# An mLSTM and sparse-attention trunk: two small products of the row scale early in the second unit, block-diagonal products behind the evacuations

## The chip, the cores and the metric

The kernel runs on one core of one Trainium2 chip. The metric is device microseconds of one execution of the whole program, from one launch. Three runs of the kernel before took 384.11, 388.54 and 380.40 us. All inputs and the output lie in device memory; the host only rearranges the weights ahead of the launch.

## The reference, cut

Two layers over 256 tokens of 1024 channels, batch 1: an mLSTM layer and a sparse-attention (NSA) layer, then a final norm. The change lies in the first third of the first layer:

```python
def rmsnorm(x, g):
    y = x * rsqrt(mean(x * x, -1) + 1e-6)          # one scale per token (row)
    return y * g

def mlstm_mixer(h, ...):                           # h = rmsnorm(x, ml_norm): 256 x 1024
    x_in, z = split(h @ w_in, 2)                   # w_in: 1024 x 4096
    x_conv = silu(conv4(x_in) + conv_b)            # causal, 4 taps
    q = headwise(x_conv, w_q)                      # blocks of 4 x 4 channels
    k = headwise(x_conv, w_k)
    v = headwise(x_in, w_v)
    gates = concat(q, k, v) @ w_if + b_if
    hh = mlstm(q, k, v, gates)                     # 4 heads of 512 channels
    return ((norm(hh) * ln_w + skip * x_conv) * silu(z)) @ w_out
```

## The kernel before

Weights are streamed. The program has one list of weight *units* (`plan`, L288); a unit is 1 MB, loaded as two halves of 512 KB each into `wr` (4 buffers, L277, issued by SyncE, SP). Each half is split into two tiles that TensorE multiplies: `wh`, a rounded copy made by ScalarE (L278, 5 buffers), and `wl`, the remainder (5 buffers). For most halves `wl` is a subtraction on VectorE (L284); for most second halves from unit 3 on, ScalarE writes the negated copy (L281) and GpSimd issues an accumulating DMA that adds `wr` to it (L282).

The activations are kept transposed, channels by tokens, and split in the same way into `hh` and `hl` (both are called hT in the trace). `project_channels` (L408) multiplies one unit: 8 channel tiles times 2 column halves times 3 products, 48 matmuls of 128x128 by 128x256 (all on L417), summed in one PSUM bank. The 16 units of `w_in` are numbered 0 to 15: units 0 to 7 give x_in (units 2h and 2h+1 belong to head h, stages A0 to A3), units 8 to 15 give z. Units 0, 1, 2, 3, 4, 5 take the banks px, px, acc1, px, px, acc1; px has two buffers, so unit 3 writes where unit 0 was, and may begin only when unit 0 has been *evacuated*.

The row scale (the rsqrt of the norm) isn't applied to the activations but behind the product: the evacuation (L444) multiplies the bank by `rb1`, the scale of each token spread over all partitions, and writes `xin`. So no evacuation can run before `rb1` is there. `norm1` (L387) makes it: VectorE sums the squares (L388), two small matmuls with a matrix of ones sum them over the partitions (L391), VectorE and GpSimd make the power -0.5 of it (L327, L329), VectorE writes it on a diagonal `dg` (L380), two small matmuls spread it (L381), and VectorE copies the bank to `rb1` (L392).

Stage B (heads_products, L491) then makes, for head h: `bdq`, the product of the folded 4x4 weights AT with a block mask from the constants `cst` (`blockdiag`, L402; one VectorE instruction on L404, written to a tile m2); the convolution (the first tap on ScalarE, L502, three on VectorE, L505; SiLU on ScalarE, L508); q by a block-diagonal matmul (L518), v likewise from `xin` with the matrix `bdv` (L525), and the scores (L532, L533). `fold` (L472) makes AT and two gate weights; the one for v goes by wtmp (L484) and a reduction (L485) into `bdv`.

What sets the order: engines work their instructions off in the order in which they stand, and that order is set when the program is built. The framework's scheduler goes by a simulated timeline of its own (schedule_with_timeline_sim): it lays an instruction in its engine's row when it deems it ready. Of the functions that are called in the order "A0 A1 B0 A2 B1 A3 B2 B3" it may thus pull pieces forward, such as four L404 instructions of later heads, as soon as AT and cst are there in its timeline. LAGS (L45) sets how far the three products of a step lie apart in a unit; for unit 1 the third follows one step behind the first.

## Time and profile before

| | |
|---|---|
| three runs | 384.11 us median (380.40 to 388.54) |
| the profiled execution | 383.82 us |
| its span, first to last instruction | 382.0 us |
| mean granted TensorE clock | 0.978 of full |

The profile is of one execution. "Idle before" in brackets is the time for which the engine of a row did nothing ahead of it, with the instruction or transfer that ended the wait as the profile infers it; where the instruction named can't be what was waited for, another ended at about the same time. A row that ends in x18 merges 18 instructions. TensorE's queue (PE) and its weight loads (PEld) are shown apart; the rows of L391, L381, L518 and L525 count two records for one matmul. The granted clock is 1.00 at 2.4 GHz and 0.50 at 1.2 GHz.

### The profile page before, as it was taken

The page shows a single profiled execution, that of the slowest core. Times are in us where ns is not written, and L with a number is a line of the kernel's source. Part 1 is how long each engine was busy: PE and PEld are TensorE (multiplying, and loading weights), DVE is VectorE, ACT ScalarE, POOL GpSimd, SP SyncE. Part 2 cuts the span into 40 slices and gives each one's busy share as a digit, 9 for nine tenths or more (in the row PEclk, how much of TensorE's full clock was granted, in tenths as well). Part 3 has the DMA queues.
Part 4 walks back from the last instruction along what each step waited for, and adds up shares of the span by engine and source line. Part 5 has one row for each costly group of instructions (what it writes and reads, how often), then busy time and mean ns, then how long its engine had stood idle before and what let it go on. Part 6 is the DMA issues. An engine that isn't in the chain of part 4 may idle for free.

```text
span 382.0 us, 6618 instructions
## 1 busy us (share of the span) xinstructions
PE 355.6 (93%) x2399; PEld 315.4 (83%) x2399; DVE 249.7 (65%) x539; ACT 242.6 (63%) x441; POOL 111.0 (29%) x151
## 2 busy tenths in 40 slices
PE   6997999999999999989987999989599899999991
PEld 6997999999998899767766899989499678777771
DVE  3979848284786789433226646799849867694325
ACT  5746877687596769365556642641869697777214
POOL 1032112230311325010113012476221834357103
PEclk9996999999999999999999999999789999999998
DMA  7899879683659796999797985546587706102002
GB/s 223 336 326 261 241 219 269 161 226 56 222 134 203 222 219 112 248 278 253 217 265 254 323 289 173 117 95 179 157 229 237 232 27 165 57 18 39 0 2 111
DMA packets 23713, 70.62 MB, mean 185 GB/s; under 512 B 2560, under 2 KB 4992, under 8 KB 23680
## 3 DMA queue, kind: packets, MB, share of 16 engines
q1 hardware_dynamic: 17552, 49.76, 38.3%
q0 software_dynamic: 4752, 16.83, 24.1%
q10 hardware_dynamic: 1376, 3.61, 2.6%
q8 instruction: 19, 0.31, 0.3%
q14 instruction: 14, 0.11, 0.1%
HBM read 51.92 MB, written 1.05 MB: 139 GB/s over the span
## 4 chain that ended last, share of the span: by engine, by line
PE 66%; DMA 14%; DVE 10%; issue 5%; ACT 3%; POOL 0%; ACTq 0%; POOLq 0%; SPq 0%; DVEq 0%
PE ps L417 30%; PE ps L727 8%; DMA wl<-wr 7%; DMA wr<-in_wo_dram 4%; DVE wl L284 2%; PE ps L941 2%; PE ps L648 2%; PE ps L929 2%; PE ps L525 2%; PE ps L1016 2%; PE ps L532 2%; PE ps L518 2%; PE ps L807 2%; PE ps L878 2%; DMA xch<-in_xt_dram 1%
## 5 line engine op out<-in xcount | busy, mean ns | idle before, releaser
L417 PE MATMUL ps<-hT,wh 128*128 128x256 f32 x832 | 140.5, 294 | 6.0 <-ACT wl L281 2.7
L417 PEld LDWEIGHTS ps<-hT,wh 128*128 128x128 f32 x832 | 122.3, 199 | 8.3 <-ACT wl L281 2.9
L278 ACT ACTIVATE wh<-wr 128x1024 fp32r<-128x1024 f32 (+2 forms) x90 | 89.5, 999 | 60.8 <-PE ps L417 29.1
L284 DVE TENSOR_TENSOR wl<-wr,wh 128x1024 fp32r<-128x1024 f32 (+2 forms) x57 | 70.0, 1229 | 36.4 <-ACT wh L278 34.1
L417 PE MATMUL ps<-hT,wl 128*128 128x256 f32 x416 | 89.5, 289 | 0.0
L417 PEld LDWEIGHTS ps<-hT,wl 128*128 128x128 f32 x416 | 67.3, 194 | 2.5 <-issue 2.1
L282 POOL DMA_DIRECT2D wl<-wr x33 | 28.9, 885 | 134.2 <-ACT wl L281 99.0
L727 PE MATMUL ps<-wh,r 128*128 128x512 f32 x128 | 41.2, 398 | 0.5 <-DVE x L749 0.5
L281 ACT ACTIVATE wl<-wr 128x1024 fp32r<-128x1024 f32 (+1 forms) x33 | 33.9, 1026 | 11.8 <-DMA wr<-in_wo_dram 6.4
L727 PEld LDWEIGHTS ps<-wh,r 128*128 128x128 f32 x128 | 24.0, 188 | 6.3 <-ACT wl L281 0.9
L727 PE MATMUL ps<-wl,r 128*128 128x512 f32 x64 | 25.7, 401 | 3.0 <-DMA wl<-wr 3.0
L505 DVE SCALAR_TENSOR_TENSOR xc<-xin,pka,xc 128x256 f32<-128x256 f32 x48 | 21.9, 510 | 1.8 <-ACT xc L502 1.8
L727 PE MATMUL ps<-wh,y 128*128 128x512 f32 x64 | 21.8, 404 | 0.0
L727 PEld LDWEIGHTS ps<-wl,r 128*128 128x128 f32 x64 | 12.0, 188 | 7.2 <-DMA wl<-wr 4.0
L807 PE MATMUL ps<-wl,hT 128*128 128x280 f32 (+1 forms) x48 | 16.8, 350 | 1.1 <-DMA wl<-wr 1.1
L806 PE MATMUL ps<-wh,hT 128*128 128x280 f32 (+1 forms) x48 | 16.0, 344 | 0.4 <-ACT wh L278 0.4
L808 PE MATMUL ps<-wh,hT 128*128 128x280 f32 (+1 forms) x48 | 16.0, 342 | 0.0
L878 PE MATMUL ps<-ka,qt 128*128 128x256 f32 (+1 forms) x32 | 12.1, 380 | 3.0 <-DVE nm L884 2.8
L727 PEld LDWEIGHTS ps<-wh,y 128*128 128x128 f32 x64 | 12.0, 189 | 3.1 <-issue 0.4
L674 POOL TENSOR_TENSOR xc<-xc,pka 128x1024 f32<-128x1024 f32 x4 | 8.8, 2206 | 18.8 <-PE ps L533 18.8
L835 POOL TENSOR_TENSOR swap<-swap,trig 128x512 f32<-128x512 f32 x6 | 9.3, 1553 | 14.8 <-DMA swap<-kraw 13.0
L444 DVE TENSOR_TENSOR xin<-ps,rb 128x512 f32<-128x512 f32 x8 | 5.4, 686 | 12.5 <-PE ps L417 12.5
(471 smaller groups left out, 660.0 us busy)
## 6 DMA issues: line engine op xcount, KB each, us to landing
wr<-in_wi_dram SPq DMA_DIRECT2D x34, 512.0 KB
wl<-wr POOLq DMA_DIRECT2D x31, 512.0 KB, 6.8
wr<-in_wo_dram SPq DMA_DIRECT2D x24, 512.0 KB
wr<-in_wi2k_dram SPq DMA_DIRECT2D x12, 512.0 KB
wr<-in_wi2z_dram SPq DMA_DIRECT2D x8, 512.0 KB
wr<-in_wi2v_dram SPq DMA_DIRECT2D x8, 280.0 KB
cw<-in_cw_dram ACTq DMA_DIRECT2D x4, 512.0 KB
xch<-in_xt_dram SPq DMA_DIRECT2D x4, 256.0 KB
```

Of the source, the lines that this page charges most:

```text
L278: A.activation(hi[:, k, :], raw[:, k, :], AF.Copy)
L281: A.activation(lo[:, k, :], raw[:, k, :], AF.Copy, scale=-1.0)
L282: GP.dma_start(out=lo[:, k, :].rearrange("p k n -> p (k n)"), in_=raw[:, k, :].rearrange("p k n -> p (k n)"), accum_op=OP.add)
L284: V.tensor_tensor(lo[:, k, :], raw[:, k, :], f32(hi[:, k, :]), op=OP.subtract)
L417: PE.matmul(ps[:, c, :], w, (hl if i == 1 else hh)[:, k, :], start=(k, c, i) == (0, 0, 0), stop=(k, i) == (KT - 1, 2), skip_group_check=True)
L505: V.scalar_tensor_tensor(xc[:, c, :], xin[:, c, tap:tap + S], tap_w(tap, c), xc[:, c, :], op0=OP.mult, op1=OP.add)
L727: PE.matmul(acc, l, r[:, k % 2, cols], start=first and i == 0, stop=last and i == 2)
L806: PE.matmul(o_, lh, hi[:, k % 2, :], start=kt == 0, stop=False)
L807: PE.matmul(o_, lh, lo[:, k % 2, :], start=False, stop=False)
L808: PE.matmul(o_, ll, hi[:, k % 2, :], start=False, stop=kt == KT - 1)
L835: (GP, V)[RE[1]].tensor_tensor(sw, sw, turn(1), op=OP.mult)
L878: PE.matmul(o_, lq, ka[:, g, :, 0:w_], start=True, stop=False)
```

## The change

Two ordering rules are added; no instruction is added, taken away or resized.

1. In unit 1, product number 8 (counted from 0) is told to stand behind the second L391 matmul on TensorE, and product number 32 behind the second L381 matmul. As a unit's products are a chain, all later ones stand behind too.
2. Each `blockdiag` instruction (L404) of head h is told to stand, on VectorE, behind the last evacuation (L444) of head h.

Both rules are order alone (NoSync): they set where an instruction may stand in its engine's row, and add no semaphore. The scheduler lays out everything else anew around them.

```diff
+EDGES = ((1, 8), (1, 32))
...
+    def behind(ins, first):
+        tc.add_manual_dep(ins.ins, first.ins.name, mybir.DependencyInfo(mybir.DependencyClass.NoSync, mybir.DependencyReason.DATA), reason="order")
...
     def token_rows(r, bank, **place):
...
-            PE.matmul(ps[:, tb * P:(tb + 1) * P], onesq, dg[:, tb, :], start=True, stop=True)
+            last[0] = PE.matmul(ps[:, tb * P:(tb + 1) * P], onesq, dg[:, tb, :], start=True, stop=True)
...
     def norm1():
...
-            PE.matmul(ps[:, tb, :], sq1[:, 0, tb * P:(tb + 1) * P], onesq[:, 0:2], start=True, stop=True)
+            sums = PE.matmul(ps[:, tb, :], sq1[:, 0, tb * P:(tb + 1) * P], onesq[:, 0:2], start=True, stop=True)
         V.tensor_copy(rb1, token_rows(rstd_of(ps[:, :, 0], D, "r1"), "ps")[0])
+        held[EDGES[0]] = sums
+        held[EDGES[1]] = last[0]
...
-    def blockdiag(src):
+    def blockdiag(src, after):
         t = T([P, 4, P], tag="m2", bufs=M2)
-        V.tensor_tensor(t.rearrange("p c (n j) -> p c n j", j=4),
+        ins = V.tensor_tensor(t.rearrange("p c (n j) -> p c n j", j=4),
                         src[:, :, None, :].to_broadcast([P, 4, 32, 4]), bm, op=OP.mult)
+        behind(ins, after)
...
         def product(k, c, i):
...
-            PE.matmul(ps[:, c, :], w, (hl if i == 1 else hh)[:, k, :], start=(k, c, i) == (0, 0, 0),
-                      stop=(k, i) == (KT - 1, 2), skip_group_check=True)
+            m = PE.matmul(ps[:, c, :], w, (hl if i == 1 else hh)[:, k, :], start=(k, c, i) == (0, 0, 0),
+                          stop=(k, i) == (KT - 1, 2), skip_group_check=True)
+            if (used[0] - 1, done_[0]) in held:
+                behind(m, held[used[0] - 1, done_[0]])
+            done_[0] += 1
...
-                V.tensor_tensor(x_, ps, spread(rb1), op=OP.mult)
+                scaled_x[h] = V.tensor_tensor(x_, ps, spread(rb1), op=OP.mult)
...
-        bdq = blockdiag(folded["AT"][:, own, :])
+        bdq = blockdiag(folded["AT"][:, own, :], scaled_x[h])
```

What the built programs make of it is shown at three places; the lines of the changed kernel are numbered 5 to 16 higher than those before (L404 is L415 there, L417 is L429, L444 is L460).

TensorE, around the two sums of squares (L391 before, L399 in the changed kernel). ps_55_265 is the bank of unit 1, ps_63_330 that of unit 2; wh_31 and wl_32 are the first half of unit 1's weights, wh_34 and wl_35 its second half, wh_40 the first half of unit 2's. Before:

```order
L417 MATMUL ps_55_265<-hT_20_113,wh_34_165 128x256
L417 MATMUL ps_55_265<-hT_19_112,wl_35_166 128x256
L391 MATMUL ps_25_143<-onesq_22_138,sq1_21_130 128x2 x2
L417 MATMUL ps_55_265<-hT_19_112,wh_34_165 128x256
L417 MATMUL ps_55_265<-hT_20_113,wh_34_165 128x256
```

In the changed kernel:

```order
L429 MATMUL ps_63_330<-hT_19_112,wh_40_178 128x256
L429 MATMUL ps_63_330<-hT_20_113,wh_40_178 128x256
L399 MATMUL ps_25_143<-onesq_22_138,sq1_21_130 128x2 x2
L429 MATMUL ps_55_265<-hT_20_113,wh_31_159 128x256
L429 MATMUL ps_55_265<-hT_19_112,wl_32_160 128x256
L429 MATMUL ps_55_265<-hT_19_112,wh_31_159 128x256
```

The sums stood behind 40 of unit 1's 48 products; now they stand behind 8 of them and 16 of unit 2's, which the scheduler pulled ahead. Between the sums and the two L381 products (L388 in the changed kernel) stand 40 products, 24 of unit 1 and 16 of unit 2; before there were 35.

VectorE, around the copy of rb1 (L392 before, L400 in the changed kernel). m2 is the block-diagonal matrix of one head, wtmp and bdv belong to the gate weight of v, wl_59 is the remainder of the first half of unit 4, xin_38 takes units 0 and 1. Before:

```order
L404 TENSOR_TENSOR m2_128_836<-AT_72_445,cst_6_70 128x512
L404 TENSOR_TENSOR m2_139_896<-AT_72_445,cst_6_70 128x512
L484 TENSOR_TENSOR wtmp_73_447<-wif_48_241,pka_7_71 128x512
L284 TENSOR_TENSOR wl_59_319<-wr_57_317,wh_58_318 128x1024
L392 COPY rb1_23_140<-ps_29_151 128x256
L485 TENSOR_REDUCE bdv_46_239<-wtmp_73_447 128x16x8
L444 TENSOR_TENSOR xin_38_175<-ps_45_189,rb1_23_140 128x2x256
```

In the changed kernel:

```order
L387 TENSOR_SCALAR dg_28_150<-pk0_1_64,r1_27_148 128x128 x2
L500 TENSOR_TENSOR wtmp_73_447<-wif_48_241,pka_7_71 128x512
L501 TENSOR_REDUCE bdv_46_239<-wtmp_73_447 128x16x8
L400 COPY rb1_23_140<-ps_29_151 128x256
L460 TENSOR_TENSOR xin_38_175<-ps_45_189,rb1_23_140 128x2x256
L484 COPY bdv_46_239<-rb1_23_140 128x1
L500 TENSOR_TENSOR wtmp_77_472<-wif_47_240,pka_7_71 128x1024
L460 TENSOR_TENSOR xin_38_175<-ps_55_265,rb1_23_140 128x2x256
L289 TENSOR_TENSOR wl_59_319<-wr_57_317,wh_58_318 128x1024
```

Four m2 products and wl_59 no longer stand ahead of rb1; wtmp_73 and its reduction still do. The m2 product of head 0 now stands behind wl_59, those of heads 1 to 3 behind their heads' evacuations, among the convolution's taps.

GpSimd, around its first accumulating DMA. r1 is the power, wl_54 the remainder of the second half of unit 3, maskt_r a mask that later stages use and that waits for cst. Before:

```order
L329 ISA
L329 TENSOR_TENSOR r1_27_148<-r1me_26_146,mhalf_12_88 128x2
L282 DMA wl_54_260<-wr_52_258 128x1024
L557 CAST maskt_r_151_958<-cst_6_70 128x256
L282 DMA wl_62_325<-wr_60_323 128x1024
```

In the changed kernel:

```order
L334 ISA
L334 TENSOR_TENSOR r1_27_148<-r1me_26_146,mhalf_12_88 128x2
L573 CAST maskt_r_151_958<-cst_6_70 128x256
L287 DMA wl_54_260<-wr_52_258 128x1024
L287 DMA wl_62_325<-wr_60_323 128x1024
```

The mask's cast and the DMA have changed places. Three more moves follow from the scheduler's new layout. On SP the 768 KB load of the rest of `bdv` (L469), which waits for a one-element copy behind rb1, now stands ahead of the load of unit 5's second half (wr_67), where before it stood behind. On ScalarE the copy rb1h and the first two convolution rows of head 0 now stand ahead of the rounded copy of unit 4's second half, and the 128 KB load of a one-hot matrix (L620) stands much later. In unit 5 the first L518 pair stands behind 18 of the 48 products, before behind 13. From there to the attention stage, at about 301 us of the span before, the rows are alike but for small exchanges in units 5 and 6; behind that, products of z, scores and values are interleaved in another order.

## Rows read from the trace of the kernel before

**Rows 1.** The page: TensorE's busy time, and its granted clock in 40 slices.

```profile
PE 355.6 (93%) x2399; PEld 315.4 (83%) x2399; DVE 249.7 (65%) x539; ACT 242.6 (63%) x441; POOL 111.0 (29%) x151
...
PEclk9996999999999999999999999999789999999998
```

**Rows 2.** Timeline of TensorE, 16 to 32 us: start us, us, what, idle before.

```profile
16.95 0.40 PE L417 MATMUL ps<-hT,wh 128*128 128x256 f32 x2
...
20.91 0.50 PE L391 MATMUL ps<-onesq,sq 128*128 128x2 f32 x4
...
27.42 1.24 PE L417 MATMUL ps<-hT,wl 128*128 128x256 f32 x9
31.35 4.18 PE L417 MATMUL ps<-hT,wh 128*128 128x256 f32 x18 [2.69 <-ACT wl L281]
```

**Rows 3.** Timeline of VectorE, 23 to 31 us.

```profile
23.36 0.48 DVE L380 TENSOR_SCALAR dg<-pk,r 128x128 f32<-128x128 f32 x2 [0.60 <-POOL r L329]
24.49 3.08 DVE L404 TENSOR_TENSOR m<-AT,cst 128x512 f32<-128x512 f32 x4 [0.65 <-DMA cst<-in_cst_dram]
27.49 0.68 DVE L484 TENSOR_TENSOR wtmp<-wif,pka 128x512 f32<-128x512 f32 x1
28.09 1.21 DVE L284 TENSOR_TENSOR wl<-wr,wh 128x1024 fp32r<-128x1024 f32 x1
29.23 0.41 DVE L392 COPY rb<-ps 128x256 f32<-128x256 f32 x1
29.56 1.04 DVE L485 TENSOR_REDUCE bdv<-wtmp 128x128 f32<-128x512 f32 x1
30.52 0.68 DVE L444 TENSOR_TENSOR xin<-ps,rb 128x512 f32<-128x512 f32 x1
```

**Rows 4.** Stretches of units 3 and 4: us; busy PE PEld DVE ACT POOL; PEclk, DMA, GB/s.

```profile
31.35:39.88 8.53, 8.53 (x48) 8.53 (x49) 7.71 (x11) 5.12 (x8) 2.45 (x5) 0.64 1.00 285
41.65:47.48 5.83, 5.83 (x51) 5.83 (x50) 5.83 (x13) 5.83 (x11) 0.12 (x1) 1.00 0.87 206
```

**Rows 5.** Timeline of GpSimd, 23 to 26 us.

```profile
23.86 1.08 POOL L282 DMA_DIRECT2D wl<-wr  x1 [0.54 <-ACT wl L281]
24.63 1.18 POOL L557 CAST maskt_r<-cst 128x256 fp32r<-128x256 f32 x1
```

**Rows 6.** DMA issues of 23 to 45 us: count, KB, median us to landing.

```profile
wl<-wr POOLq DMA_DIRECT2D x3, 512.0 KB, 9.5
bdv<-in_wvbd_dram SPq DMA_DIRECT2D x1, 768.0 KB
```

**Rows 7.** The page's DMA issues of the whole span.

```profile
wl<-wr POOLq DMA_DIRECT2D x31, 512.0 KB, 6.8
```

**Rows 8.** Timeline of ScalarE, 29 to 46 us.

```profile
29.32 1.06 ACT L278 ACTIVATE wh<-wr 128x1024 fp32r<-128x1024 f32 x1 [4.30 <-DVE wl L284]
...
35.19 1.06 ACT L278 ACTIVATE wh<-wr 128x1024 fp32r<-128x1024 f32 x1 [0.38 <-PE ps L417]
...
40.78 0.51 ACT L527 ACTIVATE v<-ps 128x408 f32<-128x408 f32 x1 [0.59 <-PE ps L525]
...
44.78 1.04 ACT L566 ACTIVATE vsp<-v 128x1024 fp32r<-128x1024 f32 x1
45.72 0.62 ACT L508 ACTIVATE xc<-xc 128x512 f32<-128x512 f32 x1
```

**Rows 9.** TensorE's waits in the whole span: us in total, times, longest us.

```profile
PE ps L727 <- DMA wl<-wr: 3.0, 3, 1.5
PE ps L878 <- DVE nm L884: 2.8, 1, 2.8
...
PE ps L381 <- ACT wh L278: 2.2, 1, 2.2
```

**Rows 10.** First output projection, and the second layer's start; columns as in rows 4.

```profile
160.00:180.00 20.00, 18.27 (x79) 14.14 (x79) 7.00 (x7) 12.33 (x15) 2.56 (x3) 1.00 0.98 267
...
200.00:220.00 20.00, 17.77 (x99) 15.04 (x98) 13.37 (x19) 12.03 (x19) 3.12 (x5) 1.00 0.89 290
```

More of the change, by code (lines that the diff above doesn't have):

```diff
@@ L62 @@
 SQP = ()
-XT = 'zt'
+EDGES = ((1, 8), (1, 32))
 XTH = 2
@@ L373, in trunk @@
     GP.memset(onesq, 1.0)
+    last = [None]
     def token_rows(r, bank, **place):
@@ L380, in token_rows @@
             V.tensor_scalar(dg[:, tb, :], ident, r[:, tb:tb + 1], None, op0=OP.mult)
-            PE.matmul(ps[:, tb * P:(tb + 1) * P], onesq, dg[:, tb, :], start=True, stop=True)
+            last[0] = PE.matmul(ps[:, tb * P:(tb + 1) * P], onesq, dg[:, tb, :], start=True, stop=True)
         return ps, dg
+    held = {}
     rb1 = T([P, S], name="rb1")
@@ L416, in product @@
             w = (lo if i == 2 else hi)[:, k % 4, c * P:(c + 1) * P]
-            PE.matmul(ps[:, c, :], w, (hl if i == 1 else hh)[:, k, :], start=(k, c, i) == (0, 0, 0),
-                      stop=(k, i) == (KT - 1, 2), skip_group_check=True)
+            m = PE.matmul(ps[:, c, :], w, (hl if i == 1 else hh)[:, k, :], start=(k, c, i) == (0, 0, 0),
[3 more added lines that the diff above has]
+            done_[0] += 1
+        done_ = [0]
         for step in range(KT + lags[1]):
@@ L436, in trunk @@
     convw = CA("convw").rearrange("p (t c) -> p t c", t=4)
-    xins, zt_ = {}, {}
+    xins, zt_, scaled_x = {}, {}, {}
     def heads_x(h):
```

## The prediction

> **What bounds the kernel now.** I read the page first. TensorE is busy for 355.6 of 382.0 us, and of its 40 slices of granted clock two places are low: the slices around 30 us, and those around 270 us [rows 1]. So a change is worth what it takes from TensorE's idle time or gives back of its clock. The timeline of TensorE shows the first place: its products run without a hole from 16.95 us on, unit 2 ends at 27.42 + 1.24 = 28.66, and then nothing is multiplied for 2.69 us, until 31.35 [rows 2]. The bracket names ScalarE's wl, but that piece belongs to a later half than the first products of unit 3 read. By the code they need the bank of unit 0, and VectorE's timeline shows that bank's evacuation at 30.52 + 0.68 = 31.20 us, just ahead of the restart [rows 3]. That evacuation is the first that rb1 lets run, and rb1 is copied only at 29.23: VectorE was first busy with four block-diagonal products (3.08 us, begun when cst landed at 24.49), wtmp (27.49) and a weight remainder (28.09 to 29.30). The diagonal dg from which rb1 comes was written already at 23.36. So rb1 waits in VectorE's row, not on its own chain.
>
> The idle time costs twice. The 48 products of unit 3 take 8.53 us at a granted clock of 0.64 on average; the 48 of unit 4 take 5.83 us at 1.00 [rows 4].
>
> **The change part by part.** No work is added; instructions change places.
>
> *The sums earlier.* In the timeline the pair at 16.95 is unit 1's products 7 and 8. After product 7 now come 16 products of unit 2, at 5.83 / 48 = 0.12 us each: the sums run at about 16.95 + 0.12 + 1.94 = 19.0 instead of 20.91 [rows 2]. Then 40 products (4.9 us) and the slot of the sums (0.5) lead to the L381 pair at 24.4. TensorE does the same work up to the end of unit 2, so that end stays at 28.66. By itself this edit frees nothing: rb1 would still wait in VectorE's row.
>
> *The block-diagonal products behind the evacuations.* This takes 3.08 us, and with the new layout the remainder's 1.21 us, from ahead of rb1. What is late next is wtmp, which needs a 256 KB load that SP issues right behind cst. The trace doesn't show when it lands: not before 24.49 (cst) and not after 27.49, when wtmp ran without a wait. At the 285 GB/s of the neighbouring stretch 256 KB take 0.9 us [rows 4], so I take 25.4. Then, at the distances of the rows: wtmp 0.60 (27.49 to 28.09), reduction 0.96 (29.56 to 30.52), rb1 0.33 (29.23 to 29.56), evacuation 0.68: it ends at 25.4 + 0.60 + 0.96 + 0.33 + 0.68 = 27.97, 0.7 us before TensorE asks for it. With wtmp at 27.49 it ends at 30.06 and 1.4 us of idle time stay. The products themselves don't vanish: each costs VectorE some 0.77 us (3.08 / 4) among later work, which I take as hidden, since VectorE now waits ahead of wtmp (dg ended at 23.84 before and ends no later now, wtmp begins at 25.4: 1.6 us) and TensorE is the busier engine; if that cover fails, it is 0.77 us for each head on the convolution's path.
>
> Worth: 2.69 us of idle time and 8.53 - 5.83 = 2.70 us of clock, together 5.4 us for TensorE at the end of unit 3.
>
> *What is given back: the accumulating DMA.* GpSimd now casts the mask first: cast at 24.63, 1.18 us, so the DMA for the second remainder of unit 3 is issued at 25.8 instead of 23.86 [rows 5]. The three DMAs of this stretch took a median of 9.5 us to land [rows 6], those of the whole span 6.8 [rows 7]. With 9.5 it lands at 35.3. TensorE reaches the last 8 of unit 3's 48 products, which read it, at 28.66 + 40 x 0.12 = 33.5. So a new wait of 1.8 us; with 6.8 there is none (32.6). I take 1.8, from the row of the same stretch. The lead is then 3.6 us, between 3.6 and 5.4.
>
> *SP's queue and ScalarE.* The 768 KB of bdv are now issued ahead of unit 5's second half [rows 6]. Before, that half had landed by 35.19, for ScalarE's copy then waited for TensorE alone [rows 8]. If it must let the 768 KB pass, that is 2.7 us at 285 GB/s: 38.0. Below it can't come sooner than before, as it is issued later; as an upper end I take 41.65, where the DMA share has fallen from 1.00 to 0.87 [rows 4] and the backlog must be gone. Behind the copy ScalarE has queued: the copy and the negated copy (1.06 each), then v, the first rows of head 1 and another weight copy (4.00 us, from 40.78 to 44.78), then SiLU of head 0 (0.62) [rows 8]: 6.74 us, so SiLU ends at 44.7, at the latest 48.4. The first L518 pair waits for it. TensorE would come to it at 47.48 - 3.6 (unit 5's start less the lead) + 18 x 0.12 = 46.1. So nothing at my value, 2.3 us at the upper end. The moves of rb1h and of two convolution rows ahead of unit 4's copy are covered by the 4.30 us for which ScalarE waited there [rows 8].
>
> A page of the Trainium skill bears on this: "DMA: Bandwidth & Descriptors", section "Queues, rings and completion order", says that on each engine descriptors are consumed in ring order. By it the load can't pass bdv, and 38.0 is the earliest, not the middle; without it SiLU would end at 41.9. The sum is the same by either, but the chance of the second rival below is larger by the rule. No row of before shows two such loads in this order.
>
> *Sum.* 383.82 - 5.4 + 1.8 = 380.2 us, against the profiled execution's own 383.82 (span 382.0 and 1.8 around it), which lies 0.3 below the median of the three runs. The likeliest case's own range is 383.82 - 5.4 = 378.4 (no wait for the DMA) to 382.5 (waits of 1.8 and 2.3).
>
> **The rivals.**
>
> *The lead is swallowed by the weight stream.* From 145 to 200 us TensorE waits for remainders three times, 3.0 us in all [rows 9], and in the output projection the DMA share is 0.98 [rows 10]. If those loads came at their own pace, an earlier TensorE would only wait longer: 383.8. Against it: each load is issued when a buffer is freed by earlier products, so it moves along.
>
> *Slower: ScalarE's row blocks L518.* If unit 5's second half lands so late that SiLU makes TensorE wait 2.69 us or more, as long as the hole that lowered the clock before, the clock falls again. The point is a landing after 46.1 + 2.69 - 6.74 = 42.0 us. The price is 2.69 + 2.70 = 5.4 us against a lead of 3.6: 385.6, and more the later it is. For it: 768 KB in pieces of 512 bytes (128 channels) stand ahead, and an accumulating DMA shares the engines. Against it: all these bytes were moved before 41.65 in the old order too.
>
> *Slower: the attention stage.* Behind 301 us another order of the same products could open one hole like the 2.8 us wait for L884 [rows 9], at whose place the clock is low too [rows 1]: with 2.70 of clock 5.5 us, 385.7. Against it: it is the only one of TensorE's waits of over 2 us that lies in that layer's work on scores, and products of several chains stand interleaved there.
>
> *The new wait lowers the clock as well.* The wait of 1.8 us in unit 3 would then cost 2.70 more: 382.9. Against it: the 2.2 us wait ahead of the second layer's L381, between 200 and 220 us, [rows 9] left the clock at 1.00 [rows 10]. [...]
>
> **How the numbers follow.** Chances: forecast 0.62, swallowed 0.12, ScalarE's row 0.10, attention 0.08, clock in unit 3 0.08. A difference of 2% (7.7 us) is about what a measurement of this kernel can tell from no change. Faster by that needs 376.1 or less, below the best case of 378.4: only the scatter of runs (380.4 to 388.5 before) or an unforeseen hole closed in the attention stage gives it, 0.13. Slower by that needs 391.5: a slow rival twice over, 0.04. Within 2%: 0.83. The range runs from 375.5 (the best case less 3 us of scatter) to 386.5 (the slow rivals and 1 us).
>
> **What would show it right or wrong.** Right: in the profile of the changed kernel the copy of rb1 stands near 27 us, unit 0's evacuation ends before unit 2 does, TensorE has no hole at 29 us and the clock is 1.00 from 30 to 38. Then the first products of unit 4 start about 3.6 us before 41.65, and the products of unit 3 show a wait for a DMA of up to 1.8 us. Wrong: a wait for SiLU in unit 5 of over 2 us; a lead at unit 5 that is gone at 200 us; or a new low slice of the clock.

## The result, and the profile after

| | before | changed |
|---|---|---|
| median of 20 runs each | 382.99 us (379.95 to 388.54) | 379.05 us (375.08 to 380.62) |
| ratio of the changed kernel to the one before | | 0.9899, 95% interval 0.9870 to 0.9928 |
| span of the profiled execution | 382.0 us | 378.7 us |

The changed kernel is faster by 2.8 to 5.0 us, within the 2% that count as no change. 380.2 was forecast. Here and in the table of the experiments the ratios leave out the runs that lie more than 1.5% above the fastest of their kernel, and the medians leave out none. The profiled execution of the changed kernel took 380.49 us, one of the longer ones of its 20 runs; a second one, profiled later (after_again below), took 377.61.

The page shows where TensorE's clock was low. Its two rows, busy time and granted clock in 40 slices:

```profile
PE 354.5 (94%) x2399; PEld 315.3 (83%) x2399; DVE 250.4 (66%) x539; ACT 242.5 (64%) x441; POOL 111.2 (29%) x151
...
PEclk9799999999999999999989999999789899999997
```

The low slice at 30 us of [rows 1] is gone; new are a 7 in the second slice, an 8 near 190 us and an 8 near 300 us. The 7 is hardly a loss against before (see the last section); the 8 near 300 us is one, and it is taken up with the rivals. The timeline of TensorE from 19 to 45 us answers to [rows 2]:

```profile
19.23 0.50 PE L399 MATMUL ps<-onesq,sq 128*128 128x2 f32 x4
...
24.45 0.61 PE L388 MATMUL ps<-dg,onesq 128*128 128x128 f32 x4
...
27.65 1.24 PE L429 MATMUL ps<-hT,wl 128*128 128x256 f32 x9
28.73 2.32 PE L429 MATMUL ps<-hT,wh 128*128 128x256 f32 x18
...
33.41 1.24 PE L429 MATMUL ps<-hT,wl 128*128 128x256 f32 x9
34.49 2.01 PE L541 MATMUL ps<-bdv,xin 128*128 128x136 f32 x16
36.25 2.40 PE L429 MATMUL ps<-hT,wh 128*128 128x256 f32 x18
...
44.25 1.02 PE L534 MATMUL ps<-xc,m 128*128 128x256 f32 x4
```

No row has a bracket: unit 2 ends and unit 3 begins at 28.73 without a hole, unit 3's last products run at 33.41 without a wait, and unit 4 starts at 36.25 instead of 41.65. VectorE's timeline, 22 to 28 us, shows why (compare [rows 3]):

```profile
22.61 0.48 DVE L387 TENSOR_SCALAR dg<-pk,r 128x128 f32<-128x128 f32 x2
25.01 0.69 DVE L500 TENSOR_TENSOR wtmp<-wif,pka 128x512 f32<-128x512 f32 x1 [1.93 <-DMA wif<-in_wif_dram]
25.74 1.11 DVE L501 TENSOR_REDUCE bdv<-wtmp 128x128 f32<-128x512 f32 x1
26.77 0.41 DVE L400 COPY rb<-ps 128x256 f32<-128x256 f32 x1
27.21 0.69 DVE L460 TENSOR_TENSOR xin<-ps,rb 128x512 f32<-128x512 f32 x1
```

VectorE now waits 1.93 us for the load of wtmp, and unit 0's evacuation is over at 27.90, 0.8 us before TensorE needs its bank. The stretch of units 3 and 4 in the windows (columns as in [rows 4]) has the full clock throughout:

```profile
28.73:36.25 7.52, 7.52 (x66) 7.52 (x65) 7.52 (x12) 4.34 (x7) 2.79 (x5) 1.00 1.03 273
36.25:42.09 5.84, 5.84 (x51) 5.84 (x50) 5.84 (x14) 5.82 (x10) 2.25 (x3) 1.00 0.98 264
```

GpSimd's timeline (compare [rows 5]) and ScalarE's (compare [rows 8]):

```profile
24.33 0.40 POOL L573 CAST maskt_r<-cst 128x256 fp32r<-128x256 f32 x1 [3.55 <-DMA cst<-in_cst_dram]
24.88 1.07 POOL L287 DMA_DIRECT2D wl<-wr  x1 [0.15 <-ACT wh L283]
```

```profile
36.10 1.06 ACT L283 ACTIVATE wh<-wr 128x1024 fp32r<-128x1024 f32 x1 [3.18 <-DMA wr<-in_wi_dram]
...
42.13 0.61 ACT L524 ACTIVATE xc<-xc 128x512 f32<-128x512 f32 x1
```

So the mask's cast took 0.40 us and the accumulating DMA behind it was issued at 24.88; the half behind the 768 KB of bdv let ScalarE go on at 36.10, and SiLU of head 0 was done at 42.74, 1.5 us before TensorE came to L534.

Where the lead went then is read from the starts of the same products in each trace (us; the second layer's first product is the 769th of L417 or L429):

| | unit 4 | first output projection | second layer | end of span |
|---|---|---|---|---|
| before | 41.65 | 150.45 | 212.75 | 382.0 |
| before_again | 41.03 | 149.84 | 213.00 | 382.5 |
| changed | 36.25 | 145.25 | 208.71 | 378.7 |
| after_again | 36.54 | 146.19 | 206.24 | 375.8 |

The lead of 5.4 us at unit 4 is 5.2 at the output projection; in the first pair 4.0 are left at the second layer and 3.3 at the end. TensorE's waits (in total, times, longest) say where the 1.2 us went (compare [rows 9]):

```profile
PE ps L743 <- DMA wl<-wr: 3.9, 3, 2.1
...
PE ps L388 <- ACT wh L283: 0.2, 1, 0.2
```

The waits for remainders in the output projection grew from 3.0 to 3.9 us, and behind the longest the clock fell. A window behind it:

```profile
189.20:192.20 3.00, 3.00 (x8) 2.32 (x8) 0.00 (x0) 2.00 (x2) 0.86 (x1) 0.50 0.93 265
```

Part of it came back at once: the 2.2 us wait ahead of the second layer's L381 became one of 0.2. Whether this loss belongs to the change is one of the questions below.

### The profile page after: what moved, and what is told of

Its sections match the earlier page's. It is cut to its first block, busy times and chain, and to the rows that moved or that the text cites. A ratio compares the mean times of both kernels' runs of the same rounds, so it can differ in the third digit from the quotient of the medians.

```text
span 378.7 us, 6629 instructions
## 1 busy us (share of the span) xinstructions
PE 354.5 (94%) x2399; PEld 315.3 (83%) x2399; DVE 250.4 (66%) x539; ACT 242.5 (64%) x441; POOL 111.2 (29%) x151
## 4 chain that ended last, share of the span: by engine, by line
PE 67%; DMA 17%; DVE 7%; issue 3%; ACT 3%; POOL 1%; POOLq 0%; ACTq 0%; SPq 0%; DVEq 0%
PE ps L429 35%; DMA wl<-wr 7%; PE ps L743 5%; DMA wr<-in_wo_dram 5%; PE ps L957 2%; PE ps L664 2%; DMA wr<-in_wi_dram 2%; PE ps L541 2%; PE ps L945 2%; PE ps L548 2%; PE ps L1032 2%; DVE wl L289 2%; PE ps L534 2%; PE ps L894 2%; DMA xch<-in_xt_dram 1%
## 5 line engine op out<-in xcount | busy, mean ns | idle before, releaser
L429 PE MATMUL ps<-hT,wh 128*128 128x256 f32 x832 | 138.7, 291 | 4.1 <-ACT wh L283 2.8
L429 PEld LDWEIGHTS ps<-hT,wh 128*128 128x128 f32 x832 | 121.0, 197 | 6.5 <-ACT wh L283 3.2
L429 PE MATMUL ps<-hT,wl 128*128 128x256 f32 x416 | 88.4, 288 | 0.0
L429 PEld LDWEIGHTS ps<-hT,wl 128*128 128x128 f32 x416 | 66.8, 193 | 1.3 <-issue 1.0
L743 PE MATMUL ps<-wh,r 128*128 128x512 f32 x128 | 42.3, 407 | 0.6 <-DVE x L765 0.6
L521 DVE SCALAR_TENSOR_TENSOR xc<-xin,pka,xc 128x256 f32<-128x256 f32 x48 | 24.0, 559 | 2.1 <-ACT xc L518 2.1
L822 PE MATMUL ps<-wh,hT 128*128 128x280 f32 (+1 forms) x48 | 16.4, 352 | 0.8 <-ACT wh L283 0.4
L824 PE MATMUL ps<-wh,hT 128*128 128x280 f32 (+1 forms) x48 | 16.4, 349 | 0.0
L743 PE MATMUL ps<-wl,y 128*128 128x512 f32 x32 | 12.7, 396 | 0.0
```

What stands on the lines that cost most here:

```text
L429: m = PE.matmul(ps[:, c, :], w, (hl if i == 1 else hh)[:, k, :], start=(k, c, i) == (0, 0, 0), stop=(k, i) == (KT - 1, 2), skip_group_chec ...
L521: V.scalar_tensor_tensor(xc[:, c, :], xin[:, c, tap:tap + S], tap_w(tap, c), xc[:, c, :], op0=OP.mult, op1=OP.add)
L743: PE.matmul(acc, l, r[:, k % 2, cols], start=first and i == 0, stop=last and i == 2)
L822: PE.matmul(o_, lh, hi[:, k % 2, :], start=kt == 0, stop=False)
L824: PE.matmul(o_, ll, hi[:, k % 2, :], start=False, stop=kt == KT - 1)
```

## The experiments

The totals, each against the kernel before on the same chip:

| kernel | median us | ratio | 95% interval |
|---|---|---|---|
| changed | 379.05 | 0.9899 | 0.9870 to 0.9928 |
| p1_sums: sums early alone | 381.80 | 0.9948 | 0.9908 to 0.9988 |
| p2_bd: block-diagonal products alone | 379.05 | 0.9873 | 0.9830 to 0.9917 |
| p1_spback: p1_sums, bdv load put back | 380.85 | 0.9955 | 0.9919 to 0.9992 |
| after_delay, 14 writes | 384.91 | 1.0061 | 1.0025 to 1.0097 |
| after_delay8, 8 writes | 383.02 | 1.0021 | 0.9983 to 1.0059 |
| after_delay5, 5 writes | 381.07 | 0.9909 | 0.9864 to 0.9953 |
| wo_before: before, lighter weight stream | 368.57 | 0.9605 | 0.9557 to 0.9653 |
| wo_after: changed, lighter weight stream | 366.01 | 0.9542 | 0.9504 to 0.9580 |
| wo_p2: p2_bd, lighter weight stream | 365.29 | 0.9567 | 0.9525 to 0.9610 |
| wo_more: changed, lighter still | 365.89 | 0.9574 | 0.9534 to 0.9615 |

### Which of the two rules does it: p1_sums and p2_bd

p1_sums, from the changed kernel:

```diff
-        behind(ins, after)
         return t
```

> The sums early (both EDGES), the block-diagonal products left where the scheduler puts them: all four again ahead of wtmp on VectorE, but without the weight remainder between wtmp and the copy of rb1. Theory A (rb1 waits in VectorE's row): the products begin when cst lands (24.3), wtmp ends near 27.9, rb1 28.3, the reduction 29.2, unit 0's evacuation 29.9; TensorE asks at 28.7, so a hole of 1.2 to 1.4 us stays in unit 3 (2.69 before). If the clock stays at 1.00 there, TensorE starts unit 4 4.0 us earlier than in the kernel before, if it falls 1.3 us earlier. Total 379 to 382 us beside 383.0 of before. Rival B (the sums' place on TensorE is what counts): no hole, unit 4 starts 5.4 us earlier, as in the changed kernel (36.25), total like the changed kernel, 379.0.

Measured: 381.80 us, ratio 0.9948. VectorE's timeline, and TensorE's at the hole and in unit 5:

```profile
24.22 2.71 DVE L415 TENSOR_TENSOR m<-AT,cst 128x512 f32<-128x512 f32 x4 [1.95 <-DMA cst<-in_cst_dram]
26.86 0.68 DVE L499 TENSOR_TENSOR wtmp<-wif,pka 128x512 f32<-128x512 f32 x1
27.46 0.41 DVE L400 COPY rb<-ps 128x256 f32<-128x256 f32 x1
27.79 1.10 DVE L500 TENSOR_REDUCE bdv<-wtmp 128x128 f32<-128x512 f32 x1
28.81 0.67 DVE L459 TENSOR_TENSOR xin<-ps,rb 128x512 f32<-128x512 f32 x1
```

```profile
29.63 0.59 PE L428 MATMUL ps<-hT,wh 128*128 128x256 f32 x3 [0.49 <-DVE bdv L483]
...
47.32 0.92 PE L533 MATMUL ps<-xc,m 128*128 128x256 f32 x3 [1.60 <-ACT xc L523]
```

The four products stand ahead of rb1 again, but the remainder of 1.21 us between wtmp and rb1 doesn't, and the products took 2.71 us instead of 3.08. TensorE, too, came to the end of unit 2 later, at 29.14 instead of 28.66. So the hole was 0.49 us, less than the 1.2 to 1.4 expected, and the clock stayed at 1.00; unit 4 began at 37.21, 4.4 us earlier than before. (p1_spback below, built with the same rule alone, had a hole of 1.45 us.) Yet the total gained only some 2 us: in units 5 and 6 TensorE waited 1.60 us for SiLU and 0.69 and 1.64 us for scores and q. At unit 7 its profiled execution (383.94 us, above its median) was 0.9 us behind the one before.

p2_bd, from the changed kernel:

```diff
-        held[EDGES[0]] = sums
-        held[EDGES[1]] = last[0]
```

> The block-diagonal products behind the evacuations, the sums left at the place that they had before. Theory A: the sums at 20.9 and the L381 pair at 25.5 are early enough, because rb1 waits for wtmp and its reduction (and here for one weight remainder of 1.2 us in between); evacuation of unit 0 ends at 28.8 at the latest, hole 0 to 0.3 us, clock 1.00 from 30 to 38, unit 4 starts 5.1 to 5.4 us earlier than before; total 378 to 380. Rival B (the sums' place counts): the hole of 2.69 us and the low clock stay, total 383.

Measured: 379.05 us, ratio 0.9873: the whole gain. The timelines of VectorE and TensorE:

```profile
25.83 0.69 DVE L498 TENSOR_TENSOR wtmp<-wif,pka 128x512 f32<-128x512 f32 x1 [1.85 <-DMA wif<-in_wif_dram]
26.44 1.22 DVE L289 TENSOR_TENSOR wl<-wr,wh 128x1024 fp32r<-128x1024 f32 x1
27.57 1.10 DVE L499 TENSOR_REDUCE bdv<-wtmp 128x128 f32<-128x512 f32 x1
28.59 0.41 DVE L400 COPY rb<-ps 128x256 f32<-128x256 f32 x1
29.04 0.69 DVE L458 TENSOR_TENSOR xin<-ps,rb 128x512 f32<-128x512 f32 x1
```

```profile
29.88 0.59 PE L427 MATMUL ps<-hT,wh 128*128 128x256 f32 x3 [1.08 <-DVE bdv L482]
```

The size was missed again: a hole of 1.08 us, where 0 to 0.3 was expected, since the load of wtmp landed at 25.8 here and a remainder stands behind wtmp. But the clock stayed at 1.00 and the lead was 4.2 us at unit 4 and 4.1 at the second layer. Theory A holds, rival B falls: with the sums at their old place rb1 still came nearly in time, because it waits for VectorE's row. The early sums remove the last 0.5 to 1.1 us of the hole (with both rules it is 0 in one profile and 0.55 us in the other, after_again), and no total shows it.

### Rival "ScalarE's row blocks L518": p1_spback

ScalarE's timeline of p1_sums shows what held SiLU up:

```profile
40.75 1.06 ACT L283 ACTIVATE wh<-wr 128x1024 fp32r<-128x1024 f32 x1 [7.04 <-DMA wr<-in_wi_dram]
```

That is unit 5's second half, behind the 768 KB of bdv on SP, as in the changed kernel. There bdv was issued at 28.00, here at 29.57, since it waits for rb1; the half came 4.65 us later. p1_spback puts the load back:

```diff
+        def part(c, dep):
+            V.tensor_copy(bdvs[:, c.start, 0:1], dep)
+            return nc.sync.dma_start(bdvs[:, c, 0:P], a["wvbd"][:, c, :])
+        part(slice(0, 4), sq1[:, 0, 0:1])
+        folded["rest"] = lambda: behind(part(slice(4, 16), rb1[:, 0:1]), loads[5, 1])
```

> The kernel with the early sums alone, and the 768 KB load of the rest of bdv put back behind the load of unit 5's second half on SP. In the kernel with the early sums alone that half reached ScalarE at 40.75 us (36.10 in the changed kernel), SiLU of head 0 ended at 47.3 and TensorE waited 1.60 us for it at 46.0 and 0.69 and 1.64 us for q at 63 to 68. Theory Q (the load waits behind the 768 KB, the mechanism of the second rival of the prediction): the half lands at 35 to 37, the wait at L518 goes and those for q shrink, the lead in unit 7 rises from -0.9 to between 2 and 4.4 us; total 378.5 to 380.5 beside 381.8. Rival L (ScalarE is late because rb1 comes 0.7 us later and more of the stream shares the engines): the half still lands near 40, the waits stay, total 381.8.

In its profile ScalarE goes on 3.6 us sooner:

```profile
37.18 1.06 ACT L283 ACTIVATE wh<-wr 128x1024 fp32r<-128x1024 f32 x1 [2.99 <-PE ps L545]
```

The bracket names a product that ended at the same moment. But the last part of the half landed at 37.08, 0.10 us ahead of the copy, and that is the distance in p1_sums and in the changed kernel too; so ScalarE still waited for the half, which came sooner. The wait at L518 is gone, waits of 0.54 and 1.39 us (for q) are left, and the lead at unit 7 is 2.0 us instead of -0.9. That is what theory Q expects, in one profile of each kernel. It is not the whole cause: in the changed kernel the half stood behind bdv as well and was used 5.2 us after its issue (30.86 to 36.10), in p1_sums 9.5 us (31.30 to 40.75), here, ahead of bdv, 6.2 us (31.01 to 37.18). What else made it late in p1_sums was not isolated. The total is not told apart: 380.85 and 381.80 us, with ratios of 0.9955 and 0.9948 whose intervals lie on each other.

### The price of a late accumulating DMA: after_delay, after_delay8, after_delay5

The prediction charged 1.8 us for this DMA, and the changed kernel paid nothing. These kernels delay it by writes to a scratch tile on GpSimd:

```diff
+DUMMY = 14   # 8, 5
...
+        scr = TS([P, 512], name="scr")
+        GP.tensor_copy(scr[:, 0:2], r1)
+        for _ in range(DUMMY):
+            idle_[:] = [GP.memset(scr, 0.0)]
...
+                    if (len(loaded), i) in ((3, 1), (4, 1)):
+                        behind(ins, idle_[0])
+                        idle_[:] = [ins]
```

and hold units 4 to 6 and the v products of head 0 behind unit 3. The next accumulating DMA, of unit 4, stands behind this one.

> The changed kernel with 14 writes of a scratch tile on GpSimd ahead of the accumulating DMA for the second remainder of unit 3 (issued near 28 instead of 24.88), and the products of unit 3 held ahead of those of units 4 and 5 and of the v products, so that TensorE can't go round them. In the changed kernel that DMA landed 1.5 us before TensorE asked for it (31.9 against 33.4). Theory D (the step of the prediction was right in kind, only the landing was off): landing at 28 + 7.0 = 35.0, a wait of 1.3 to 2.2 us at the last 8 products of unit 3, unit 4 starts 1.3 to 2.2 us later than 36.25, clock 1.00; total 380 to 381.5. Rival C (the wait lowers the clock too): another 1 to 2.7 us, total 382 to 384. Rival N (the bytes come no later, because the DMA engines are the limit): landing by 33.4, no wait, 379.

Measured: 384.91 us. Each write took 0.58 us, the DMA was issued at 31.77, later than meant, and TensorE waited 4.94 us; the clock was low behind it and unit 4 started at 43.49, 7.2 us later than in the changed kernel. More than theory D or rival C allowed, because the delay was larger; N falls.

> As the kernel with the delayed accumulating DMA, but with 8 writes of the scratch tile instead of 14: at 0.58 us each the DMA of unit 3 is issued near 28.3 us (24.88 in the changed kernel, 31.77 with 14). Everything else stands in nearly the same order as in the changed kernel. Theory D (each microsecond of wait costs one, the clock falls only at the longer ones): landing 28.3 + 4.8 to 7.4 = 33.1 to 35.7, wait 0 to 2.3 us, clock 1.00 behind it, unit 4 starts 0 to 2.3 us later than 36.25 and the total is 379 to 381.3. Rival C (any such wait lowers the clock): up to 2.7 us more, unit 4 up to 5 us later, total up to 384.

Measured: 383.02 us. GpSimd's timeline, TensorE's, and the window behind the wait:

```profile
28.17 1.07 POOL L288 DMA_DIRECT2D wl<-wr  x1
```

```profile
37.43 1.99 PE L439 MATMUL ps<-hT,wl 128*128 128x256 f32 x8 [4.30 <-DMA wl<-wr]
...
41.81 2.41 PE L439 MATMUL ps<-hT,wh 128*128 128x256 f32 x18
```

```profile
37.60:41.00 3.40, 3.40 (x17) 3.40 (x18) 2.26 (x5) 1.22 (x2) 0.00 (x0) 0.51 1.00 286
```

From issue to TensorE's restart it is 9.26 us, near the 9.5 of [rows 6]. The time of issue doesn't explain it: from issue to landing the same DMA took 9.5 us in the kernel before (issued at 23.86), 7.0 and 8.5 in the two profiles of the changed kernel (24.88 and 25.14), 10.1 in p2_bd (23.76), 9.1 here and 6.3 with 14 writes (31.77). What sets it was not isolated. From the end of the wait at 37.43 to unit 4 it took 4.38 us, where the changed kernel took 2.84 (33.41 to 36.25): the low clock cost 1.5 us on top of the wait of 4.30. The lead is eaten up, in the profile and in the total.

> As before with 5 writes of the scratch tile: TensorE's and ScalarE's rows are those of the changed kernel, the accumulating DMA of unit 3 is issued near 26.4 us. With 8 writes it was issued at 28.17 and TensorE went on 9.3 us later, after a wait of 4.30 us, and the clock was low for half a unit. Theory D (a wait near the 1.8 us that the prediction foresaw costs itself and no clock): TensorE goes on at 26.4 + 7.0 to 9.3 = 33.4 to 35.7, a wait of 0 to 2.3 us, unit 4 starts by just that later than 36.25 (start of TensorE's first product taken out), total 379 to 381.3. Rival C (it lowers the clock): 1 to 2.7 us more on top of a wait of over 1 us, total 381 to 384.

Measured: 381.07 us, ratio 0.9909. TensorE's and ScalarE's rows stand as in the changed kernel, the DMA was issued at 25.95:

```profile
33.76 1.19 PE L439 MATMUL ps<-hT,wl 128*128 128x256 f32 x8 [1.10 <-DMA wl<-wr]
...
36.55 2.40 PE L439 MATMUL ps<-hT,wh 128*128 128x256 f32 x18
...
45.37 0.92 PE L546 MATMUL ps<-xc,m 128*128 128x256 f32 x3 [0.67 <-ACT xc L536]
```

```profile
38.80 1.06 ACT L284 ACTIVATE wh<-wr 128x1024 fp32r<-128x1024 f32 x1 [6.31 <-PE ps L439]
...
44.70 0.62 ACT L536 ACTIVATE xc<-xc 128x512 f32<-128x512 f32 x1
```

The wait of 1.10 us cost itself alone: from 33.76 to unit 4 it is 2.79 us, at the full clock. That is theory D, though the total lies where the ranges of both theories meet. What nobody expected stands behind it: ScalarE's copy of the late half began at 38.80 (the bracket names a product, but the half's last part landed at 38.70), SiLU ended at 45.32, TensorE waited 0.67 us for it and then 1.57, 0.83 and 0.57 us more for q and scores. The kernel was 0.3 us behind the changed one at unit 4 and 4.8 us at unit 7. TensorE's order there is the changed kernel's, row for row. The half was issued at 30.43, sooner than in the changed kernel (30.86), and used 8.4 us later instead of 5.2; what slowed it was not isolated.

### Is the lead lost in the output projection: wo_after, wo_before, wo_p2, wo_more, and both kernels again

```diff
+WO_DVE = (18, 19, 20, 21, 22, 23)
-BY_DMA = [(i, 1) for i in list(range(24)) + list(range(24, 48, 2)) if i not in NOT_POOL] + [(i, 0) for i in BOTH]
+BY_DMA = [(i, 1) for i in list(range(24)) + list(range(24, 48, 2)) if i not in NOT_POOL + WO_DVE] + [(i, 0) for i in BOTH]
```

> The changed kernel, with the remainders of the second halves of the last six weight pieces of the first output projection taken by VectorE instead of the accumulating DMAs (six DMAs of 512 KB less between 145 and 195 us). Theory W (the lead of 5.2 us is lost because the weight stream of that stage is at its limit): the waits for wl in that stage (3.9 us) and the low clock behind the longest of them (1.7 us lost) go, and the lead at the start of the second layer is 5 us or more; total 373.5 to 376. Rival V (VectorE's remainder, which must wait for ScalarE's rounded copy, comes no earlier than the DMA): waits for VectorE take their place, total 378 to 380. Rival T: the time is gained there and given back by TensorE's waits at the start of the second layer, total 377 to 379.

> The same edit to the kernel before: remainders of six halves of the first output projection by VectorE. Theory W: the 3.0 us of waits for wl go, total 380; the distance between this kernel and the same edit of the changed kernel is then 5.2 us (the full lead of unit 4) instead of 3.9. Rival T: the distance stays at 3.9 or less. Rival V: 383, as before.

Measured: 366.01 and 368.57 us. Both are far faster than expected. TensorE's waits in wo_after name no remainder in the whole span, and a window of the stage shows the DMA share at 0.57 where it was 0.98 in [rows 10]:

```profile
160.00:180.00 20.00, 20.00 (x92) 16.16 (x91) 10.49 (x12) 10.23 (x14) 0.00 (x0) 1.00 0.57 187
```

That is theory W, and more: from the projection's start to the second layer's the lead on the changed kernel grows from -0.5 to 8.5 us (200.25 against 208.71), where the waits and the clock had been worth 5.6. The other 7.5 of the 16 us between the spans (378.7 and 362.7) arise behind the second layer's start, where the scheduler put the products into another order; by the page TensorE is busy for 8.4 us less in the whole span (346.1) and idle for 7.6 us less. What that order gains was not followed up.

The pair answers the question only in part. At unit 4 the two kernels are 4.5 us apart (40.03 and 35.51), at the projection 3.1 (148.83 and 145.76), at the second layer 4.0, at the end 3.9; the medians are 2.6 apart. So in this pair of profiles nothing is lost from the projection to the end without the full stream. What is lost, 1.4 us, is lost in units 5 and 6.

> The block-diagonal products behind the evacuations, the sums where they stood before, and six remainders of the first output projection by VectorE. With the weight stream out of the way a difference in the first units should reach the end. If the early sums add what they showed in unit 3 (a hole of 1.08 us with the block-diagonal edit alone, none with both): 367.1, beside 366.0 with both. If they add nothing: 366.0. If their new order later on costs: 364 to 365.

Measured: 365.29 us, ratio 0.9567. With a hole of 1.59 us ahead of unit 3, which left the clock at 1.00, it is no slower than wo_after; the early sums add nothing that can be measured.

> The changed kernel with all eleven accumulating DMAs of the first output projection's eight weight pieces replaced by VectorE's remainders (six before). Theory W: in that stage no wait was left after six, so nothing more is gained: 366 give or take 1. Rival S (the DMA engines were still the limit ahead of the stage and in the second layer's first weights): 363 to 365. Rival V (five more remainders of 1.2 us each stand in VectorE's row in front of the evacuations of z): 367 to 369.

```diff
-BOTH = (15, 16, 17)
+BOTH = ()
+WO_DVE = (16, 17, 18, 19, 20, 21, 22, 23)
```

One of the eleven belongs to the last unit of z, just ahead of the stage. Measured: 365.89 us: nothing more, as theory W said.

> The changed kernel once more, unaltered. Theory W (its lead is lost in the first output projection because the weight stream is at its limit there): again a wait of about 2 us for a remainder between 180 and 195 us, and a lead of about 4 us at the second layer's start. Rival E (that loss belongs to one execution): the waits there are under 1.5 us each, no low clock, and the lead at the second layer's start is about 5 us.

Measured: 377.61 us. Unit 3 has a hole in this execution, and the accumulating DMA is waited for (it landed at 33.61, though the bracket names ScalarE):

```profile
28.35 2.39 PE L429 MATMUL ps<-hT,wh 128*128 128x256 f32 x18 [0.55 <-DVE bdv L484]
...
33.75 1.19 PE L429 MATMUL ps<-hT,wl 128*128 128x256 f32 x8 [0.37 <-ACT wh L283]
```

TensorE ended unit 2 at 27.80, 0.9 us sooner than in the first profile, and unit 0's evacuation ended at 28.20: behind the load of wtmp, which let VectorE go on at 25.30, rb1 is again what TensorE waits for. The lead at unit 4 is 4.5 us here. Its waits for remainders in the projection:

```profile
PE ps L743 <- DMA wl<-wr: 2.0, 2, 1.3
```

and the window from 180 to 200 us, where the first profile had 0.91:

```profile
180.00:200.00 20.00, 20.00 (x89) 16.28 (x88) 8.72 (x11) 11.92 (x17) 2.34 (x3) 1.00 0.96 267
```

> The kernel before once more, unaltered, to have two executions of each. Theory W and rival E alike: the hole of 2.5 to 2.8 us ahead of unit 3 with the low clock behind it is there again; the waits for remainders in the first output projection add up to 2 to 4 us.

Measured: 384.24 us, a hole of 3.27 us ahead of unit 3, and 4.0 us of waits in the projection with the clock low behind two of them. Rival E holds: the 1.2 us lost there belonged to one execution. In the second pair the lead at the projection is 3.7 us and grows to 6.8 at the second layer and 6.7 at the end. In the ten profiles with the full stream, of all these kernels, the way from the projection's start to the second layer's takes 60.1 to 63.5 us, 63.5 and 60.1 in the two of the changed kernel alone. So this stage differs by up to 3.4 us from one execution to the next; no fixed price of the change is seen in it.

## Why the prediction was right or wrong

*What bounds the kernel* was read rightly. rb1 waited in VectorE's row: p2_bd, which moves nothing but the block-diagonal products, has the whole gain, and p1_sums, which leaves them ahead of rb1, gained some 2 us in the median (the two intervals meet at 0.991).

*The sums earlier*: forecast 19.0 for the sums and 24.4 for the L381 pair, measured 19.23 and 24.45. That this rule frees nothing by itself did not hold for the program that the scheduler builds: alone, it also takes the remainder from ahead of rb1, so p1_sums had a hole of 0.49 us only, began unit 4 4.4 us sooner than before, and lost that lead in units 5 and 6.

*The block-diagonal products behind the evacuations*: wtmp at 25.01 (25.4), rb1 at 26.77 (27.0), evacuation over at 27.90 (27.97), hole gone, clock 1.00 from 28.73 on, 5.4 us ahead at unit 4 (5.4). Each of these came out within 0.4 us in the first profile. In the second a hole of 0.55 us and a lead of 4.5 us show that the 0.7 us to spare was less than executions differ by.

*What is given back* is the step that failed: "So a new wait of 1.8 us; with 6.8 there is none (32.6). I take 1.8, from the row of the same stretch." No wait was measured in the first profile and 0.37 us in the second. Both sizes were too large. The cast's 1.18 us in [rows 5] were measured right behind a DMA's issue on the same engine; ahead of it the cast took 0.40, and the DMA was issued at 24.88, not 25.8. That takes half of the 1.8 us away. And the 9.5 us are the median of three DMAs of a stretch; this one needed 7.0 us in the first profile and 8.5 in the second. Since it needed 6.3 to 10.1 us in the ten profiles, the other half is as much luck of the execution as error. The end of the range named for it, 0, was nearly the right one. The delayed kernels show that the kind was right: from an issue at about 25 us on TensorE waits for this DMA.

*SP's queue and ScalarE*: landing at 36.1 (38.0), SiLU over at 42.74 (44.7), L518 at 44.25 (46.1), wait 0 (0). The 6.74 us from the copy to the end of SiLU were 6.64. The step took 2.7 us for letting the 768 KB pass, on top of 35.19, and that sum was too late by 1.9 us: the bdv load itself was issued at 28.00 instead of 31.29, since rb1 came sooner, and the half was used 5.2 us after its issue. The rival built on it failed in its price. From a copy at 42.0 on, SiLU was to make TensorE wait 2.69 us, and the clock would fall. Four traces with the load behind bdv give the copy's start, SiLU's end and TensorE's wait for it: 36.10, 42.74, 0 in the changed kernel; 37.44, 43.95, 0 in after_again; 38.80, 45.32, 0.67 in after_delay5; 40.75, 47.26, 1.60 in p1_sums. By these TensorE begins to wait at a copy of about 38, the clock stays at 1.00 as far as 40.75, and more waits follow: q and the scores come late too, and with 0.67 us for SiLU all of them are 3.6. The changed kernel stands some 0.6 to 2 us from that point. The Trainium skill, "DMA: Bandwidth & Descriptors", section "Queues, rings and completion order", has descriptors consumed in ring order on each engine; p1_spback agrees, where the half put ahead of bdv was used at 37.18 and not at 40.75, but the 5.2 us that it took behind bdv in the changed kernel show that the order alone doesn't make it late.

*The sum* of 3.6 us of gain met the measured 3.9 (2.8 to 5.0), but not by its own terms. The give-back wasn't paid; 5.2 us arrived at the output projection in the first pair and 3.7 in the second, and what the stages from there on leave differs from run to run: 3.3 us in the first pair, 6.7 in the second. So that 380.2 was near 379.05 is in part luck: a term that wasn't paid stood in for losses that were not in the sum, and what these are on average two pairs of profiles don't show.

*The other rivals.* "Swallowed by the weight stream" named the right stage: the lighter stream made the two kernels 15 and 13 us faster. As a fixed loss of the lead it falls with after_again. "The attention stage" came in small. No new hole opened, but a wait that the kernel before has too now lowers the clock. The first products behind it, before and changed:

```profile
301.55 2.42 PE L417 MATMUL ps<-hT,wh 128*128 128x256 f32 x18 [1.22 <-DVE z L961]
```

```profile
298.36 3.74 PE L429 MATMUL ps<-hT,wh 128*128 128x256 f32 x18 [1.23 <-DVE z L977]
```

The granted clock is 1.00 there before and 0.50 in the changed kernel, and the second profile of each is alike (2.42 and 3.67 us). That is the 8 near 300 us, a new low slice of the clock, which the prediction had named as a sign of being wrong. It costs 1.3 us. The new order behind it is worth about as much: from these products to the end it is 80.5 us in both profiles of before, 80.3 in both of the changed kernel, and 79.0 in p1_sums and after_delay5, which have TensorE's order of the changed kernel there and kept the clock up. So from the second layer's start to the end the lead fell by only 0.7 us in the first pair and by 0.1 in the second. "The new wait lowers the clock as well": not at 1.10 us; at 4.30 us 1.5 us on top. A wait of 1.8 us at this place was not run. The Trainium skill, "TensorE: Matmul & The Clock Gate", section "HAM oscillation — how this bites in real kernels", tells of a kernel whose waits for a DMA, of about 3 to 5 us each, re-throttled the array; the runs agree at 4.30 and 4.94 us, and 1.10 us is no such wait.

A version beats both kernels clearly: wo_p2 and wo_after, at 365.3 and 366.0 us (ratios 0.9567 and 0.9542). They take six remainders of the first output projection from the DMA engines, which were full, and give them to VectorE, which was busy for 7.0 of 20 us there [rows 10]. About half of what that gives arises behind that stage, in a new order of the products, and is not explained.

## What to carry to other kernels

A result that many wait for (here a row scale that frees the first bank) should be looked for in its engine's row, not on its own chain: what stood ahead of it was work that nobody needed yet, and moving that alone was the whole gain. A lead won early is only kept by stages that have slack; before looking for two or three more microseconds in front, take load from the stage whose transfers are at their limit. And when a load slips past another on a queue, follow the whole row behind it: a wait of 0.7 us was followed by 3.0 us of waits for the operands that were late next.

## What the runs showed that was not expected

The length of a wait didn't say alone whether the clock fell. In the first units waits of 0.49, 1.08, 1.10, 1.45 and 1.59 us left it at 1.00 and those of 2.69, 3.27, 3.89, 4.30 and 4.94 us lowered it. In later stages 1.74, 1.88 (before_again) and 2.14 us (changed kernel), all in the output projection, lowered it, and 2.23 us (the kernel before, second layer's L381) did not. The wait of 1.2 us ahead of the products of z lowered it in both profiles of the changed kernel and in neither of the kernel before.

The granted clock of a profile can miss its first stretch. From 9.80 to 13.40 us both kernels ran 19 products in 3.60 us, at the pace of the half clock; the window of the kernel before says 1.00, that of the changed kernel 0.50:

```profile
9.80:13.40 3.60, 3.60 (x19) 3.60 (x19) 3.60 (x8) 3.60 (x8) 0.00 (x0) 1.00 1.04 407
```

```profile
9.80:13.40 3.60, 3.60 (x19) 3.60 (x19) 3.60 (x8) 3.60 (x7) 0.00 (x0) 0.50 1.04 416
```

So most of the new 7 in the second slice was there before too: unit 2 begins at 22.53 instead of 22.30. And the mean clocks of the two profiles (0.978 and 0.966) can't be compared.

An order that is the same row for row on TensorE can still lose 4.5 us from unit 4 to unit 7: after_delay5 against the changed kernel, where an accumulating DMA was issued 1.1 us later. The unaltered kernel itself lost 0.7 us there in its second profile against its first, so how much of it is the DMA's is not shown. What the later DMA does delay is a load: the accumulating DMA reads a buffer of `wr`, and in the changed kernel SP issued the load that follows unit 5's second half at 31.93, right behind the DMA's landing at 31.91, in after_delay5 at 33.64 behind 33.62.
